# A hybrid RWKV-7 / pooling decoder block on one core: each step's leftover work queued behind the next weight split, GpSimd's DMAs in program order, and five products in 512/256-column pairs

## The chip, the cores and the metric

The kernel runs on one core of a Trainium2 chip. A core has TensorE (PE in the profile, its weight loads PEld), VectorE (DVE), ScalarE (ACT), GpSimd (POOL) and SyncE (SP), each with its own instruction queue, and 16 DMA engines that all of these queues feed. The metric is device microseconds of one execution, the median of the runs made.

## The reference, cut to what matters

One decoder block on a (1, 512, 2048) input in float32: 512 tokens, 2048 channels, 5632 hidden channels in the MLP (44 tiles of 128).

```python
h = _rmsnorm(x, norm1_g) * (1 + sc1) + sh1
p = h @ w_in                                  # RWKV-7 heads and pooling heads
mix = concat([rwkv7(p), pool(p)]) @ w_out
x = x + gt1 * mix
h = _rmsnorm(x, norm2_g) * (1 + sc2) + sh2
u = h @ w_up                                  # (512, 2 * 5632)
y = conv_b + sum_j conv_w[j] * shifted(u, j)  # causal, width 3
val, gate = split(y, 2)
x = x + gt2 * ((silu(gate) * val) @ w_down)
return _rmsnorm(x, norm_f_g)
```

The change is in the last part alone: `h @ w_up` ("up") and `... @ w_down` ("down"). Products are made to nearly full float32 precision: each operand is split into a rounded part and the rest ("hi" and "lo"), and hi·hi, hi·lo and lo·hi are summed.

## The kernel before

**A product.** `wsplit` (lines 1382 to 1390) splits a weight tile of 128 x 1024: ACT casts the hi part (line 1388), DVE subtracts to get the lo part (line 1389). There are three buffers for split weights, used in turn, so the hi cast of the third tile from now waits until PE is done with the present one. `mm3` (lines 132 to 150) then issues three matmuls for each 128 rows of the contraction: hi·hi (line 136), hi·lo (137), lo·hi (138). A product over 8 row tiles is 24 matmuls. With 256 columns (half of the tokens, `H0` or `H1`) they are called 128x256, with all tokens 128x512. `mm2` (lines 1217 to 1219), used in the output projection, instead issues two for each row tile: one of 512 columns with hi weights against hi and lo side by side, and one of 256 with lo weights. Its two halves of the PSUM bank are then added by whoever reads it.

**Up.** 44 pairs of output tiles, each a Strassen-Winograd 2 x 2 product of seven half-width products (`product`, line 1392). Thirty-four of the pairs form `w12 · Y21` themselves; `order` (line 1614) lists the pairs, and `n` is the place in that list. DVE is also used for the sums `r2`, `r4` and for the convolution, ACT for copies out of PSUM ("cap") and the activation.

**Down.** A list of steps (`Step`, line 1678) which `pipeline` (line 1683) runs: for step i it issues the step's matmuls, the weight load of step i+4, the split of step i+2, and then the step's `after` list (PSUM reads, operand preparation, stores, DMA loads). The framework's scheduler then orders the instructions of each engine by its own estimate; the program text is not the order. The steps are, in turn:
- 16 *plain* rows (`plain_steps`, line 1752): output tile f, first 8 hidden tiles, 24 matmuls of 512 columns; the last pair's open product is the second step. Beside them `operands` (line 1537) builds the Winograd operands Y11, Y21, Y22, T1, T2; `last_operand` builds T3 and T4 at the end of these rows, from the same buffers (xa, xb) that the second group's weights are loaded into.
- 8 *groups* f = 0..7 (`group_steps`, line 1781) over the next 16 hidden tiles, each of seven half-width steps of 24 matmuls: Y11, (T4 of the group before), Y21, T1, T2, Y22, T3. After them stand p1 to p7: p1 and p4 copy the first PSUM bank into `cap` (lines 1806 and 1816), p3 (line 1813) copies the second one, into which Y22 is then added, p2, p5 and p6 add on DVE, p7 copies on ACT; p5 and p7 also send the result to DRAM with an accumulating DMA from GpSimd's queue (lines 1820, 1830). The weights of a group are two loads of 1 MB on SP's queue (line 1779, `wd4`), issued by `pair_load`.
- *rest* rows (`rest_steps`) over the last 20 hidden tiles in blocks of 8, 8 and 4, first four rows block by block, then four rows, then two times eight rows of half width. Their activations are loaded by `rest_load` (line 1514; the first four by GpSimd's queue, the others by SP's) into the group operands' buffers as these come free, and split by `rest_split` (ACT line 1519, DVE line 1520). `fetch_x2` (lines 1905 and 1907) loads the residual and the sum stored so far on GpSimd's queue, `join_x2` (DVE, line 1910) adds them, `gate_row` (line 1890) makes the last modulation vector by DVE, `finish` writes the normalised output.

Of the kernel before, what the change touches and what calls it, by code (L numbers as in the profile page):

```python
# [1 line left out]

# [1 line left out]

# [5 lines left out]
F32 = mybir.dt.float32  # L10
# [3 lines left out]
ALU = mybir.AluOpType  # L14
PSUM = bass.MemoryType.PSUM

P = 128
T = 512
# [7 lines left out]
WC = 512  # L26
NWF = 8
NSLOT = 10
LA = 4
NB = 10  # L30
NA = 4
# [37 lines left out]
def block_kernel(ctx, tc, a, out, stop=None, dbg=None):  # L69
    nc = tc.nc  # L70
# [1139 lines left out]
    def bank():  # L1210
        return psm.tile([P, T], F32, tag="b", name="b")
# [20 lines left out]
    def x2(f, sl=slice(0, T)):  # L1232
        return x2q[f // 4][:, f % 4, sl]
# [143 lines left out]
        def done(self):  # L1377
            free.append(self.home)

    nsplit, lo_of = [0], [None]  # L1380

    def wsplit(src, off=0):
        n = src.shape[-1]
        i = nsplit[0] % 3
        nsplit[0] += 1
        w = (ea, ea, ub)[i].tile([P, WS], F32R, tag=f"w{i}", name="uw")
        hi, lo = w[:, off : off + n], w[:, 2 * QW + off : 2 * QW + off + n]
        S.copy(hi, src)  # L1388
        lo_of[0] = V.tensor_tensor(lo, src, hi.bitcast(F32), op=ALU.subtract)  # L1389
        return hi, lo  # L1390

    def product(ps, w, Y, start=True):
        wh, wl = wsplit(w, 16)
        n = w.shape[-1] // P
        for k in range(n):
            sl = slice(k * P, (k + 1) * P)
            y = Y[k // 4]
            mm3(ps, wh[:, sl], wl[:, sl], y[:, 0, k % 4, :], y[:, 1, k % 4, :], start=start and k == 0,
                stop=k == n - 1, more=not start)

    def row(n, pool, tag):
        t = pool.tile([P, 4 * QW], F32, tag=tag, name="wrow")
# [106 lines left out]
    def rest_load(i, eng):  # L1509
        u, g = REST[i]  # L1510
        pool, tag = UNITS[u][g]
        t = pool.tile([P, 2, 2, T], F32R, tag=tag, name="act2")
        for n in range(2):
            eng.dma_start(t[:, 1, n, :].bitcast(F32), ad[3 * ND + 2 * i + n])
        A3.extend([t[:, :, n, :] for n in range(2)])

    def rest_split(i):
# [99 lines left out]
    for n, j in enumerate(order):  # L1617
# [13 lines left out]
        if j < NB:  # L1631
            u1 = Slot("u1")
            nc.sync.dma_start(u1.t, early[j])
        else:
            product(pa, w11, Y11)
            S.copy(cap[:, H0], pa)
            if pend:
                last_product(pend)
            u1 = Slot("u1")
            pb = bank()[:, 0:HT]  # L1640
            product(pb, w12, Y21)
            V.tensor_add(u1[:, H0], cap[:, H0], pb)
        ahead_of_down(j)
        u2 = Slot("u2")
        pc = bank()[:, 0:HT]
# [37 lines left out]
    def pipeline(steps):  # L1683

        def ahead(i, what):
            if i < len(steps):
                what(steps[i])

        def load(st):
            if st.load:  # L1690
                st.load()

        def split(st):
            st.w = wsplit(st.raw(), st.off)

        for i in range(LA):
            ahead(i, load)
        ahead(0, split)
        ahead(1, split)
        carried = []  # L1700
        for i, st in enumerate(steps):
            st.mm(*st.w)
            ahead(i + LA, load)
            ahead(i + 2, split)
            todo, carried = carried + ([] if st.hold else st.after), st.after if st.hold else []
            for fn in todo:
                fn()

    def products(ps, wh, wl, Y, n, start=True):
        for k in range(n):  # L1710
# [70 lines left out]
    def group_steps():  # L1781

        out_, before = [], None
        for f in range(NWF):
# [42 lines left out]

            def p7(d=d, f=f):
                S.activation(d["u2"][:, H0], d["a"], AF.Copy, scale=-1.0)
                G.dma_start(yd[f + NWF], d["u2"].t, accum_op=ALU.add)  # L1830
                d["u2"].done()

            out_.append(Step(w11, mul(d, "a", "Y11"), [p1], off=16))
# [67 lines left out]
    def fetch_x2(f):  # L1901
        if not x2q:
            x2q.extend(quad(i, "x2") for i in range(4))
            accs.append(Slot("acc").t)
        G.dma_start(x2(f), x2d[f])
        parts[f] = Slot("yd")
        G.dma_start(parts[f].t, yd[f])

    def join_x2(f):
        V.scalar_tensor_tensor(x2(f), parts[f].t, gate(f), x2(f), op0=ALU.mult, op1=ALU.add)  # L1910
# [29 lines left out]
    for b, (k0, n) in enumerate(BLOCKS):  # L1940
        for f in range(4):
            st = four[f][0][b]
            steps.append(st)
            if b == 0 and f == 0:
                st.after += [lambda i=i: rest_load(i, nc.sync) for i in (4, 5)]
                before.after.append(gate_begin)
                steps.append(before)
            if b == 0 and f == 1:
                st.after += [lambda i=i: rest_load(i, nc.sync) for i in (6, 7)]
            if b == 0 and f == 2:  # L1950
                st.after += [lambda i=i: rest_split(i) for i in (4, 5)]
            if b == 0 and f == 3:
                st.after += [lambda i=i: rest_split(i) for i in (6, 7)] + [lambda i=i: rest_load(i, nc.sync) for i in (8, 9)]
# [135 lines left out]
```

## Time and profile before

| what | value |
|---|---|
| three runs | 2159.04, 2160.34, 2186.05 us; median 2160.34 us |
| the profiled execution: its own time | 2156.44 us |
| the profiled execution: its span in the trace | 2154.7 us (1.74 us less) |
| PE busy in the span | 2110.4 us, 98% |
| DVE, ACT, POOL busy | 78%, 49%, 11% |
| mean granted PE clock | 0.992 |
| up pairs run from about | 880 to 1668 us |
| plain rows, groups, rest rows from about | 1668, 1758 and 1916 us |
| last matmul of the rest rows, end | about 2138 us, 2154.7 us |

How to read it: a matmul record is longer than the distance to the next one, since matmuls overlap in the array; what a matmul costs is the distance of starts. In a window's row the number behind x is the count of instructions, PEclk the granted TensorE clock as a share of full speed, and in a timeline or wait row the bracket holds the engine's idle time before an instruction and what ended it.

### The profile page before, as it was taken

How to read it: one execution, taken by the hardware profiler on the slowest of the kernel's cores; microseconds unless marked ns; L12 is line 12 of the kernel's file. 1: busy time of each engine (PE TensorE's matmuls, PEld its weight loads, DVE VectorE, ACT ScalarE, POOL GpSimd, SP SyncE). 2: the span in 40 equal slices, each digit the busy share in tenths (PEclk: the TensorE clock that was granted, in tenths of full speed). 3: DMA queues.
4: the chain of work that ended last, by engine and by line, in shares of the span. 5: the costliest groups of instructions: out<-in, count | busy, mean ns of one | idle time of the engine just before them, and what ended most of it. 6: DMA issues, size and time to landing. Idle time of an engine off the chain costs nothing.

```text
span 2154.7 us, 44008 instructions
## 1 busy us (share of the span) xinstructions
PE 2110.4 (98%) x17864; PEld 1866.6 (87%) x17864; DVE 1677.5 (78%) x2615; ACT 1047.0 (49%) x1510; POOL 236.5 (11%) x376
## 2 busy tenths in 40 slices
PE   7999999999999999999999999999999999999997
PEld 3567777777767888999999999999999889988897
DVE  7988898988854677888888878777788657757764
ACT  4354444443433466655555555555556444443353
POOL 0002122221100101100100000000000000120000
PEclk9999999999999999999999999999999999999998
DMA  9966665665537565989889877777777635697855
GB/s 393 413 213 198 199 199 173 199 178 184 149 109 262 189 197 179 293 247 261 245 244 261 229 211 208 203 207 211 210 210 212 214 114 147 166 318 267 293 187 166
DMA packets 169485, 471.89 MB, mean 219 GB/s; under 512 B 21361, under 2 KB 29505, under 8 KB 159169
## 3 DMA queue, kind: packets, MB, share of 16 engines
q1 hardware_dynamic: 120370, 352.12, 48.0%
q0 software_dynamic: 27696, 79.20, 17.5%
q10 hardware_dynamic: 21216, 37.76, 5.8%
q8 instruction: 140, 2.29, 0.4%
q14 instruction: 63, 0.52, 0.1%
HBM read 432.81 MB, written 36.18 MB: 218 GB/s over the span
## 4 chain that ended last, share of the span: by engine, by line
PE 86%; DVE 5%; DMA 4%; ACT 2%; issue 2%; POOL 0%; DVEq 0%; ACTq 0%; POOLq 0%; SPq 0%
PE b L138 19%; PE b L136 19%; PE b L137 19%; PE mm L646 11%; PE pf L427 4%; PE b L1218 2%; PE b L1219 1%; DVE war L765 1%; PE pb L1048 1%; DMA wrow<-wup 1%; DMA war<-ada 1%; DMA wa<-ada 1%; PE pa L712 1%; DMA al<-ad 0%; ACT x L1318 0%
## 5 line engine op out<-in xcount | busy, mean ns | idle before, releaser
L138 PE MATMUL b<-t,uw 128*128 128x256 f32 x1408 | 388.6, 276 | 0.0
L136 PE MATMUL b<-t,uw 128*128 128x256 f32 x1408 | 388.6, 276 | 0.0
L137 PE MATMUL b<-t,uw 128*128 128x256 f32 x1408 | 388.6, 276 | 0.0
L136 PE MATMUL b<-y,uw 128*128 128x256 f32 x1056 | 293.2, 278 | 2.2 <-ACT uw L1388 2.2
L138 PE MATMUL b<-y,uw 128*128 128x256 f32 x1056 | 292.7, 277 | 0.9 <-DVE uw L1389 0.7
L646 PE MATMUL mm<-ahl,whi 128*128 128x512 f32 x864 | 290.6, 410 | 2.0 <-DVE rk L549 1.4
L137 PE MATMUL b<-y,uw 128*128 128x256 f32 x1056 | 292.5, 277 | 0.0
L137 PEld LDWEIGHTS b<-t,uw 128*128 128x128 f32 x1408 | 264.3, 188 | 0.0
L136 PEld LDWEIGHTS b<-t,uw 128*128 128x128 f32 x1408 | 264.3, 188 | 0.0
L138 PEld LDWEIGHTS b<-t,uw 128*128 128x128 f32 x1408 | 264.3, 188 | 0.0
L1389 DVE TENSOR_TENSOR uw<-r,uw 128x1024 fp32r<-128x1024 f32 x164 | 200.4, 1222 | 78.3 <-ACT uw L1388 78.3
L1389 DVE TENSOR_TENSOR uw<-wquart,uw 128x1024 fp32r<-128x1024 f32 x156 | 190.6, 1222 | 67.9 <-ACT uw L1388 67.5
L1389 DVE TENSOR_TENSOR uw<-wd,uw 128x1024 fp32r<-128x1024 f32 (+1 forms) x112 | 124.0, 1108 | 109.1 <-ACT uw L1388 109.1
L1388 ACT CAST uw<-wquart 128x1024 fp32r<-128x1024 f32 x156 | 164.0, 1051 | 88.3 <-PE b L138 65.3
L1388 ACT CAST uw<-r 128x1024 fp32r<-128x1024 f32 x164 | 172.5, 1052 | 61.2 <-PE b L138 61.1
L138 PE MATMUL b<-act,uw 128*128 128x256 f32 (+1 forms) x608 | 200.4, 330 | 1.4 <-DVE uw L1389 1.4
L136 PEld LDWEIGHTS b<-y,uw 128*128 128x128 f32 x1056 | 198.9, 188 | 2.8 <-ACT uw L1388 2.8
L136 PE MATMUL b<-act,uw 128*128 128x256 f32 (+1 forms) x608 | 200.6, 330 | 0.0
L138 PEld LDWEIGHTS b<-y,uw 128*128 128x128 f32 x1056 | 199.0, 189 | 1.7 <-DVE uw L1389 1.7
L137 PE MATMUL b<-act,uw 128*128 128x256 f32 (+1 forms) x608 | 200.4, 330 | 0.0
L137 PEld LDWEIGHTS b<-y,uw 128*128 128x128 f32 x1056 | 199.1, 189 | 0.1
L646 PEld LDWEIGHTS mm<-ahl,whi 128*128 128x128 f32 x864 | 158.8, 189 | 43.3 <-issue 12.2
(356 smaller groups left out, 4596.5 us busy)
## 6 DMA issues: line engine op xcount, KB each, us to landing
wquart<-wup SPq DMA_DIRECT2D x176, 512.0 KB, 5.3
wa<-ada SPq DMA_DIRECT2D x48, 1024.0 KB, 9.4
war<-ada SPq DMA_DIRECT2D x192, 256.0 KB, 3.8
wd<-wdn SPq DMA_DIRECT2D x64, 512.0 KB, 4.5
wraw<-win ACTq DMA_DIRECT2D x118, 256.0 KB, 4.1
wraw<-wout SPq DMA_DIRECT2D x96, 256.0 KB, 3.5
wquart<-wup POOLq DMA_DIRECT2D x44, 512.0 KB, 6.8
r<-wup SPq DMA_DIRECT2D x44, 512.0 KB, 4.6
```

The costliest lines, as they stand in the source:

```text
L136: muls = [lambda: PE.matmul(ps, wh, xh, start=start, stop=False, skip_group_check=more), lambda: PE.matmul(ps, wh, xl, start=False, stop=F ...
L137: lambda: PE.matmul(ps, wh, xl, start=False, stop=False, skip_group_check=more),
L138: lambda: PE.matmul(ps, wl, xh, start=False, stop=stop, skip_group_check=more)]
L427: PE.matmul(pf[n % 2 * 4 + ii], w[:, sl], full[k], start=k == 0, stop=k == KT - 1)
L646: PE.matmul(ps, w[:, sl], x, start=first, stop=k == KT - 1 and i == 2)
L712: PE.matmul(ps, pw[:, i, d * P : (d + 1) * P], zs[i], start=i == 0, stop=i == 1)
L765: V.scalar_tensor_tensor(wa, wa, 1.0, cqs[kq], op0=ALU.mult, op1=ALU.mult, accum_out=modq[:, kq, j : j + 1])
L1048: PE.matmul(pt[HS[e], h, c * 2 * L : (c + 1) * 2 * L], nt[HS[e], s, :], rw[HS[e], s, :, :], start=True, stop=True)
L1218: PE.matmul(ps[:, :].rearrange("p (a b) -> p a b", a=2), wh, x, start=start, stop=False)
L1219: PE.matmul(ps[:, 0:HT], wl, x[:, 0, :], start=False, stop=stop)
L1388: S.copy(hi, src)
L1389: lo_of[0] = V.tensor_tensor(lo, src, hi.bitcast(F32), op=ALU.subtract)
```

## The change

- In `pipeline`, everything in a step's `after` list is issued with an edge behind the hi cast and the lo subtraction of the last split made (that of step i+2): on ACT nothing of it stands before that cast, on DVE nothing before that subtraction. The edge orders instructions on the same engine; it is no wait on another one.
- All GpSimd DMAs of the down part go through `queue`, which puts each behind the one before it in program order.
- In five pairs (n = 0, 2, 6, 14, 28, which are j = 10, 11, 13, 17 and 28) the second product uses `mm2`: 8 matmuls of 512 columns and 8 of 256 instead of 24 of 256, and two DVE additions instead of one.

```diff
+WIDE = (0, 2, 6, 14, 28)
...
-        S.copy(hi, src)
+        hi_of[0] = S.copy(hi, src)
...
+    def product_wide(ps, w, Y):
+        wh, wl = wsplit(w, 16)
+        for k in range(w.shape[-1] // P):
+            sl = slice(k * P, (k + 1) * P)
+            mm2(ps, wh[:, sl], wl[:, sl], Y[k // 4][:, :, k % 4, :], k == 0, k == 7)
...
-            pb = bank()[:, 0:HT]
-            product(pb, w12, Y21)
-            V.tensor_add(u1[:, H0], cap[:, H0], pb)
+            pb = bank()
+            if n in WIDE:
+                product_wide(pb, w12, Y21)
+                V.tensor_add(u1[:, H0], cap[:, H0], pb[:, HT:T])
+                V.tensor_add(u1[:, H0], u1[:, H0], pb[:, 0:HT])
+            else:
+                product(pb[:, 0:HT], w12, Y21)
+                V.tensor_add(u1[:, H0], cap[:, H0], pb[:, 0:HT])
...
+    def queue(*args, **kw):
+        with tc.issue_after(g_of[0].ins) if g_of[0] else nullcontext():
+            g_of[0] = G.dma_start(*args, **kw)
...
-            for fn in todo:
-                fn()
+            with tc.issue_after(hi_of[0].ins), tc.issue_after(lo_of[0].ins):
+                for fn in todo:
+                    fn()
...
-        G.dma_start(yd[f], s_.t)
+        queue(yd[f], s_.t)
...
-                G.dma_start(yd[f], d["u1"].t, accum_op=ALU.add)
+                queue(yd[f], d["u1"].t, accum_op=ALU.add)
...
-        p[0].after += [lambda: rest_load(0, G), lambda: rest_load(1, G)]
-        p[2].after += [lambda: rest_load(2, G), lambda: rest_load(3, G)]
+        p[0].after += [lambda: rest_load(0, queue), lambda: rest_load(1, queue)]
+        p[2].after += [lambda: rest_load(2, queue), lambda: rest_load(3, queue)]
...
-        G.dma_start(x2(f), x2d[f])
+        queue(x2(f), x2d[f])
         parts[f] = Slot("yd")
-        G.dma_start(parts[f].t, yd[f])
+        queue(parts[f].t, yd[f])
```

Other GpSimd DMAs of the down part are changed in the same way. Lines of the changed kernel are 7 to 17 higher there. What this does to the built order is seen at three places. In the rows, `uw` is a split weight tile, the number behind a name tells buffers' uses apart.

**ACT, last group (f = 7) of the down part.** `b_21432` (before) and `b_21397` (changed) are the bank that p3 reads, `act2` the rest activations, `u2` p7 of group 6; r2, r4, r3 are the weights of T2, Y22 and T3. Before:

```order
L1388 CAST uw_21389<-r1_21387 128x1024
L1519 CAST act2_21357<-act2_21357 128x512 x2
L1829 ACTIVATE u2_21325<-b_21113 128x256
L1388 CAST uw_21421<-r2_21419 128x1024
L1519 CAST act2_21360<-act2_21360 128x512 x2
L1388 CAST uw_21461<-r4_21459 128x1024
L1519 CAST act2_21426<-act2_21426 128x512 x2
L1519 CAST act2_21429<-act2_21429 128x512
L1813 COPY cap_21355<-b_21432 128x256
L1388 CAST uw_21495<-r3_21493 128x1024
```

With the change:

```order
L1389 CAST uw_21354<-r1_21352 128x1024
L1846 ACTIVATE u2_21290<-b_21078 128x256
L1389 CAST uw_21386<-r2_21384 128x1024
L1389 CAST uw_21426<-r4_21424 128x1024
L1526 CAST act2_21322<-act2_21322 128x512 x2
L1830 COPY cap_21320<-b_21397 128x256
L1389 CAST uw_21460<-r3_21458 128x1024
L1526 CAST act2_21325<-act2_21325 128x512 x2
```

Ahead of p3's copy stood seven casts of rest activations, now two stand there, and p7 of group 6 (`u2`) stands ahead of all of them.

**GpSimd's queue at the same place.** `ad` are the rest activations in DRAM, `x2d` the residual. Before:

```order
L1820 DMA yd6_19188<-u1_21204 128x512
L1905 DMA x2_21801<-x2d8_7428 128x512
L1905 DMA x2_21801<-x2d9_7429 128x512
L1905 DMA x2_21801<-x2d10_7430 128x512
L1514 DMA act2_21357<-ad24_9801 128x512
L1514 DMA act2_21357<-ad25_9802 128x512
L1514 DMA act2_21360<-ad26_9803 128x512
L1514 DMA act2_21360<-ad27_9804 128x512
L1905 DMA x2_21801<-x2d11_7431 128x512
L1830 DMA yd14_19196<-u2_21325 128x512
L1514 DMA act2_21426<-ad28_9805 128x512
```

With the change:

```order
L1692 DMA yd6_19153<-u1_21169 128x512
L1692 DMA act2_21322<-ad24_9801 128x512
L1692 DMA act2_21322<-ad25_9802 128x512
L1692 DMA act2_21325<-ad26_9803 128x512
L1692 DMA act2_21325<-ad27_9804 128x512
L1692 DMA yd14_19161<-u2_21290 128x512
L1692 DMA act2_21391<-ad28_9805 128x512
```

The residual's loads have left the stretch ahead of the activations' loads; they now stand in pairs with the `yd` loads behind the last accumulating store.

**PE, ACT and DVE at the start of the second group (f = 1).** Before, PE goes from T3 of group 0 straight through Y11 of group 1 (`b_20043`), and ACT casts in the order Y11, T4, Y21:

```order
L137 MATMUL b_19834<-T3_19875,uw_19981 128x256
L138 MATMUL b_19834<-T3_19875,uw_19981 128x256
L136 MATMUL b_20043<-Y11_19370,uw_20009 128x256
L137 MATMUL b_20043<-Y11_19370,uw_20009 128x256
L138 MATMUL b_20043<-Y11_19370,uw_20009 128x256
```

```order
L1816 COPY cap_19878<-b_19834 128x256
L1388 CAST uw_20009<-wd4_19920 128x1024
L1388 CAST uw_20038<-wd4_19681 128x1024
L1388 CAST uw_20068<-wd4_19920 128x1024
L1806 COPY cap_20071<-b_20043 128x256
```

With the change, on PE, on ACT and on DVE (`wd4_19885` is the load with the weights of Y11 and Y21 of group 1, `r2_20094` a sum for its T2):

```order
L139 MATMUL b_19799<-T3_19840,uw_19946 128x256
L137 MATMUL b_20008<-Y11_19335,uw_19974 128x256
L138 MATMUL b_20008<-Y11_19335,uw_19974 128x256
L137 MATMUL b_20069<-Y21_19338,uw_20033 128x256
L138 MATMUL b_20069<-Y21_19338,uw_20033 128x256
L139 MATMUL b_20008<-Y11_19335,uw_19974 128x256
```

```order
L1833 COPY cap_19843<-b_19799 128x256
L1389 CAST uw_20003<-wd4_19646 128x1024
L1389 CAST uw_19974<-wd4_19885 128x1024
L1389 CAST uw_20033<-wd4_19885 128x1024
L1823 COPY cap_20036<-b_20008 128x256
```

```order
L1809 TENSOR_TENSOR r1_20062<-wd4_19887 128x1024
L1390 TENSOR_TENSOR uw_20003<-wd4_19646,uw_20003 128x1024
L1809 TENSOR_TENSOR r2_20094<-r1_20062,wd4_19885 128x1024
L1390 TENSOR_TENSOR uw_19974<-wd4_19885,uw_19974 128x1024
L1836 TENSOR_TENSOR u1_19880<-cap_19843,b_19889 128x256
```

T4's weights (`uw_20003`) are now split ahead of Y11's (`uw_19974`) on both engines, and two matmuls of Y21 (`b_20069`) stand between the second and the third matmul of Y11. DVE's order further ahead has the parts of T3 and T4 later than before: the subtraction of T4's second half, which frees the buffer of `wd4_19885`, stands behind the split of T2's weights and p2 of group 0:

```order
L1390 TENSOR_TENSOR uw_19829<-r1_19827,uw_19829 128x1024
L1539 TENSOR_TENSOR T3_19835<-t3_19448,T3_19835 128x512
L1539 TENSOR_TENSOR T3_19835<-t3_19450,T3_19835 128x512
L1809 TENSOR_TENSOR r3_19944<-wd4_19644,wd4_19646 128x1024
L1539 TENSOR_TENSOR T3_19840<-xb_19293,T3_19840 128x1024
L1539 TENSOR_TENSOR T4_19845<-t4_19489,T4_19845 128x512
L1539 TENSOR_TENSOR T4_19845<-t4_19491,T4_19845 128x512
L1390 TENSOR_TENSOR uw_19877<-r2_19875,uw_19877 128x1024
L1827 TENSOR_TENSOR u1_19880<-cap_19843,b_19850 128x256
L1539 TENSOR_TENSOR T4_19882<-xa_19292,T4_19882 128x1024
```

Before, T4's last subtraction was done ahead of the split of T2's weights, and five of the others ahead of the split of T1's.

More of the change, by code (lines that the diff above doesn't have):

```diff
@@ L1 @@
-from contextlib import ExitStack
+from contextlib import ExitStack, nullcontext
 import numpy as np
@@ L1378, in done @@
             free.append(self.home)
[L1380 removed]
+    nsplit, lo_of, hi_of, g_of = [0], [None], [None], [None]
     def wsplit(src, off=0):
@@ L1829, in p7 @@
                 S.activation(d["u2"][:, H0], d["a"], AF.Copy, scale=-1.0)
-                G.dma_start(yd[f + NWF], d["u2"].t, accum_op=ALU.add)
+                queue(yd[f + NWF], d["u2"].t, accum_op=ALU.add)
                 d["u2"].done()
@@ L1944, in block_kernel @@
             if b == 0 and f == 0:
-                st.after += [lambda i=i: rest_load(i, nc.sync) for i in (4, 5)]
+                st.after += [lambda i=i: rest_load(i, nc.sync.dma_start) for i in (4, 5)]
                 before.after.append(gate_begin)
@@ L1948, in block_kernel @@
             if b == 0 and f == 1:
-                st.after += [lambda i=i: rest_load(i, nc.sync) for i in (6, 7)]
+                st.after += [lambda i=i: rest_load(i, nc.sync.dma_start) for i in (6, 7)]
             if b == 0 and f == 2:
@@ L1952, in block_kernel @@
             if b == 0 and f == 3:
-                st.after += [lambda i=i: rest_split(i) for i in (6, 7)] + [lambda i=i: rest_load(i, nc.sync) for i in (8, 9)]
+                st.after += [lambda i=i: rest_split(i) for i in (6, 7)] + [lambda i=i: rest_load(i, nc.sync.dma_start) for i in (8, 9)]
             if b == 1 and f in (0, 2):
```

2 lines of the change are left out of this document (1 added, 1 removed).

## The prediction

> **What bounds the kernel now.** The page first: who is busy, and which chain of work ended last.
>
> ```profile
> PE 2110.4 (98%) x17864; PEld 1866.6 (87%) x17864; DVE 1677.5 (78%) x2615; ACT 1047.0 (49%) x1510; POOL 236.5 (11%) x376
> PE 86%; DVE 5%; DMA 4%; ACT 2%; issue 2%; POOL 0%; DVEq 0%; ACTq 0%; POOLq 0%; SPq 0%
> ```
>
> TensorE is busy nearly throughout. A change of order can therefore bring only the places where PE stands still or runs at a lower clock, and can cost only where it makes new ones. So next the waits of PE, of which three rows lie in the up and down parts:
>
> ```profile
> PE b L136 <- ACT cap L1813: 4.6, 1, 4.6
> PE b L136 <- ACT uw L1388: 2.2, 3, 1.0
> PE b L138 <- DVE uw L1389: 2.1, 2, 1.4
> ```
>
> The columns are total us, times, longest. The longest of the third row is where the plain rows begin, the first row is in the last group. Windows show both, the stretch behind the second, and some that I need for prices:
>
> ```profile
> core 0: us, PE busy (x) PEld busy (x) DVE busy (x) ACT busy (x) POOL busy (x), PEclk, DMA share, GB/s
> 740.00:790.00 50.00, 50.00 (x286) 43.47 (x285) 35.60 (x65) 25.78 (x46) 4.67 (x9) 1.00 0.66 209
> 853.00:856.00 3.00, 1.52 (x9) 1.11 (x8) 3.00 (x4) 2.11 (x3) 0.03 (x1) 0.94 0.95 352
> 856.00:859.00 3.00, 3.00 (x16) 3.00 (x16) 3.00 (x4) 0.00 (x0) 1.43 (x2) 0.50 0.67 184
> 868.00:871.00 3.00, 1.55 (x9) 1.11 (x9) 3.00 (x4) 1.89 (x2) 0.54 (x1) 1.00 0.97 395
> 900.00:1600.00 700.00, 700.00 (x6179) 700.00 (x6178) 575.53 (x673) 389.26 (x506) 69.05 (x79) 1.00 0.83 227
> 1660.00:1670.00 10.00, 8.61 (x72) 8.13 (x71) 8.76 (x11) 8.12 (x13) 0.00 (x0) 1.00 0.74 220
> 1690.00:1750.00 60.00, 60.00 (x266) 49.71 (x265) 27.01 (x25) 19.03 (x25) 5.98 (x12) 1.00 0.46 161
> 1908.00:1914.00 6.00, 5.91 (x28) 5.91 (x29) 4.04 (x6) 4.97 (x10) 0.00 (x0) 0.52 0.99 373
> ```
>
> In a window without waits, 256-column matmuls start every 700/6179 = 0.1133 us and those of 512 columns every 60/266 = 0.2256 us. Everything below is priced against these.
>
> **Part 1: the wait at the first plain row.** DVE, then ACT, at 1660 to 1670 us:
>
> ```profile
> 1665.99 0.41 DVE L1662 TENSOR_TENSOR u<-cap,b 128x256 f32<-128x256 f32 x1
> 1667.65 0.69 DVE L1505 TENSOR_TENSOR act<-al,act 128x512 fp32r<-128x512 f32 x1 [1.24 <-ACT act L1504]
> 1668.26 1.22 DVE L1389 TENSOR_TENSOR uw<-wd,uw 128x1024 fp32r<-128x1024 f32 x1
> ```
>
> ```profile
> 1664.06 1.06 ACT L1388 CAST uw<-wd 128x1024 fp32r<-128x1024 f32 x1
> 1667.00 0.62 ACT L1504 CAST act<-al 128x512 fp32r<-128x512 f32 x1 [1.88 <-DMA al<-ad]
> ```
>
> The hi half was ready at 1665.1, but DVE's lo half stood behind a subtraction whose activation came late by DMA. In the changed order that lo half stands ahead of it, and DVE was free at 1666.4. **−1.39 us** (10 − 8.61). Bounds: −1.39 (nothing is left to gain) and 0, if the late activation then holds up the next row's lo half; I take the whole, since this row's 24 matmuls give 24 × 0.2256 = 5.4 us of cover.
>
> **Part 2: the wait in the last group.** PE, ACT and POOL:
>
> ```profile
> 1908.09 0.58 PE L136 MATMUL b<-Y,uw 128*128 128x256 f32 x1 [4.63 <-ACT cap L1813]
> ```
>
> ```profile
> 1896.02 1.31 ACT L1519 CAST act<-act 128x512 fp32r<-128x512 f32 x2 [2.08 <-DMA act<-ad]
> 1897.24 0.38 ACT L1829 ACTIVATE u<-b 128x256 f32<-128x256 f32 x1
> ...
> 1899.78 1.04 ACT L1388 CAST uw<-r 128x1024 fp32r<-128x1024 f32 x1
> 1905.03 0.62 ACT L1519 CAST act<-act 128x512 fp32r<-128x512 f32 x1 [4.21 <-DMA act<-ad]
> ...
> 1907.15 0.62 ACT L1519 CAST act<-act 128x512 fp32r<-128x512 f32 x1 [0.39 <-DMA act<-ad]
> 1907.67 0.37 ACT L1813 COPY cap<-b 128x256 f32<-128x256 f32 x1
> ```
>
> ```profile
> 1889.78 1.64 POOL L1905 DMA_DIRECT2D x<-x2d  x3 [0.96 <-DVE uw L1389]
> 1891.52 1.09 POOL L1514 DMA_DIRECT2D act<-ad  x2
> ...
> 1897.91 0.89 POOL L1830 DMA_DIRECT2D yd<-u  x1 [3.41 <-ACT u L1829]
> 1898.48 2.48 POOL L1514 DMA_DIRECT2D act<-ad  x4
> ```
>
> The circle reads: Y22's first matmul waits for p3's copy; that copy stands behind three casts whose loads arrive at 1905 to 1907; the loads were issued at 1898.48, behind the store of p7, which waited for the ACT copy at 1897.24, which in turn stood behind casts that waited for the first loads. With the change p7's copy stands ahead of all these casts. It needs only its bank and can run about 2 us earlier, near 1895.3, so the last two pairs' loads are issued at about 1896.7 to 1899. The first four loads start about 1.5 us earlier, the three x2d issues (1.64 us) no longer being ahead of them. Ahead of p3's copy now stand the split of Y22's weights and two casts, both of the first pair (issued near 1891.5, landing some 4 us later). The copy then comes at about 1900.8 and Y22 needs it at 1903.46. **−4.63 us.** Bounds: −4.63, and 0 if those two casts still end last. I take the former; 2.7 us lie between copy and need.
>
> **Part 3: the clock behind it.** In 1908:1914 PE ran 28 matmuls in 5.91 us at a granted clock of 0.52; at the normal pitch these take 28 × 0.1133 = 3.17. **−2.74 us**, if the wait goes; 0 if it stays.
>
> The Trainium skill, "TensorE: Matmul & The Clock Gate", section "Part 1: The HAM clock gate (the "warmup" mystery)", has the clock fall to half after an idle window of about 3.4 us and return after about 3.4 us of activity. This trace differs twice: low clock lasted some 5.5 us here, and it also came in 856:859 when only 1.48 of the 3 us ahead were idle. By the page's 3.4 us this term would be an estimated −1.7 rather than −2.74.
>
> **Part 4: a wait that the new order makes.** At f = 1 the changed order lets three things come late. T4's subtraction (`T<-xa`), which frees the buffer of the next load of weights, moves behind the split of T2's weights. Then T4's split stands ahead of Y11's on ACT and DVE, and on DVE a sum (`r2`) that needs the late load also stands ahead of Y11's lo half. Before, DVE and ACT had there:
>
> ```profile
> 1763.16 1.22 DVE L1532 TENSOR_TENSOR T<-xa,T 128x1024 fp32r<-128x1024 f32 x1
> ...
> 1771.87 1.23 DVE L1792 TENSOR_TENSOR r<-r,wd 128x1024 f32<-128x1024 f32 x1 [1.80 <-DMA wd<-wdn]
> 1773.02 1.22 DVE L1389 TENSOR_TENSOR uw<-wd,uw 128x1024 fp32r<-128x1024 f32 x1
> ```
>
> ```profile
> 1764.41 0.33 SPq L1779 DMA_DIRECT2D wd<-wdn  x1
> ```
>
> ```profile
> DMA to landing us min/median/max: 4.9/6.0/7.4
> ```
>
> ```profile
> 1771.86 2.13 ACT L1388 CAST uw<-wd 128x1024 fp32r<-128x1024 f32 x2 [1.22 <-DMA wd<-wdn]
> ```
>
> ```profile
> 1775.46 0.28 PE L136 MATMUL b<-Y,uw 128*128 128x256 f32 x1
> ```
>
> T3 of group 0 ends and Y11 of group 1 begins at 1775.46. In the changed order `T<-xa` ends about 1769, the load is issued then instead of at 1764.41, and lands 6.0 us later at about 1775.1. `r2` then runs 1775.2 to 1776.4, Y11's lo half up to 1777.55. In PE's order only two matmuls of Y11 and two of Y21 stand ahead of the one that needs that lo half, 4 × 0.1133 = 0.45 us, up to 1775.91. So PE stands still 1777.6 − 1775.91 = **+1.7 us**. With a landing of 4.9 `r2` is ready at 1774.0 and only T4's own lo half (1774.05 to 1775.28) precedes: 0.6 us; with 7.4 it is +2.9. Below that 0, if `T<-xa` comes earlier than I reckon. I take the median's. T4's split needs the third buffer back from Y22, whose end leaves 1.3 us for its cast; that is met in either order.
>
> **Part 5: five wide products.** The price is in the output projection, where pairs of 512 and 256 columns run: 50 us / 143 pairs = 0.3497 per pair, against 3 × 0.1133 = 0.3399. Difference 0.0098 × 8 row tiles × 5 products = **+0.39 us**. From the other side, single matmuls give 0.2256 + 0.1133 = 0.3389, so −0.04. I take the pair's row, the nearest. The five extra additions on DVE (below, 413 ns each, 2.1 us) fall where DVE idles for ACT's casts:
>
> ```profile
> L1389 DVE TENSOR_TENSOR uw<-wquart,uw 128x1024 fp32r<-128x1024 f32 x156 | 190.6, 1222 | 67.9 <-ACT uw L1388 67.5
> ...
> L1642 DVE TENSOR_TENSOR u<-cap,b 128x256 f32<-128x256 f32 x34 | 14.1, 413 | 0.1
> ```
>
> Without that cover they would cost up to 5 × 0.41 = 2.1 us.
>
> **Part 6: what moves at no cost.** All other steps' leftovers (PSUM reads, operand casts, stores, SP's loads) shift by at most a split, 1.22 us on DVE, behind work that PE needs one or two products later (24 × 0.1133 = 2.7 us each). The edges make no engine wait for another; what lies behind them is read a step later. On POOL's queue x2d and yd loads now come in pairs behind the last accumulating store, near 1917; the first join is needed later than that. After the last matmul (2138 us) nothing moves.
>
> **Sum**, in the profiled execution: −1.39 − 4.63 − 2.74 + 1.7 + 0.39 = −6.67 us, 2156.44 → 2149.8. That execution lies 3.9 us below the median of the runs, 2160.34; carried over, the forecast is **2153.7 us**. By the terms' bounds: lowest −8.76 − 0.04 = −8.8, so 2151.5; highest with all chosen gains and the dear ends +2.9 and +2.5, −3.4, so 2157.0. With a run's scatter of 0.5 us its own range is 2151 to 2157.5.
>
> **The rivals.** *A dip at f = 1.* For it: 1.48 us of idle in 853:856 was followed by half clock (16 matmuls in 3 us, 3 − 16 × 0.1133 = 1.19 us lost). Against it: 1.45 us idle in 868:871 brought none, nor did 1.39 at 1668 us. With a landing of 7.4 (+1.2) and a dip of 1.2 to 2.7: about 2156.8 us.
>
> *The last group's wait stays.* Two casts of loaded activations still stand ahead of p3's copy. If the first pair of loads lands some 6 us later than reckoned, behind the group's weight loads (the engines' DMA share is 0.99 there), ACT is held as before, the copy is late and the clock falls: +4.63 + 2.74, so 2161.1 us, slightly slower than before.
>
> *Strict order on GpSimd's queue delays the joins.* A yd load waits for a slot that the previous join frees:
>
> ```profile
> POOL yd L1907 <- DVE x L1910: 59.8, 8, 15.1
> ```
>
> Before, an x2d load of the next row could go ahead of such a wait; now it queues behind, so a join may find its residual not there and hold the splits behind it on DVE. It decides once a load takes longer than the distance from slot to join; at about 1 us for each of 12 rows, 2165.7 us. Against it: the slot was waited for up to 15.1 us, so rows are far apart.
>
> *No wait at f = 1*, since DVE reaches `T<-xa` a step earlier: 2152.0 us.
>
> **How the numbers follow.** Forecast 0.5, dip at f = 1 0.2, last group's wait stays 0.1, joins late 0.1, no wait at f = 1 0.1. The range 2146 to 2164 us holds all but the late joins and half of what scatters beyond the others, about 8 in 10. Two per cent, 43 us, is about what a measurement of this kernel can tell from no change. No case comes near it: faster 0.01, same 0.97, slower 0.02 (joins that stall for 4 us a row).
>
> **What would show it.** Right: no row of PE waiting for p3's copy; full clock behind 1900 us; one new wait of 1 to 3 us for a lo split 110 us behind the first plain row; pairs in the wide products near 0.35 us. Wrong: PE waiting in the groups f = 2 to 7, in the rest rows for a split held by a join, or in the up part behind the extra additions.

## The result, and the profile after

| | before | changed |
|---|---|---|
| median of 9 runs each | 2160.34 us | 2184.24 us |
| lowest to highest | 2156.03 to 2190.92 us | 2182.59 to 2191.46 us |
| profiled execution: own time, span | 2156.44, 2154.7 us | 2186.87, 2185.1 us |

The ratio is 1.0104, with a 95% interval of 1.0069 to 1.0139. The forecast of 2153.7 us was missed by 30.5 us and the end of its range (2164) by 20: the change was to save some 7 us and costs about 24, or 1%. One thing in these rows matters for what follows: two of the nine runs of before lie at 2186 and 2191 us, in the band of the changed kernel, and not one run of the changed kernel lies lower.

The page of the changed kernel, the rows of busy time and of the chain:

```profile
PE 2141.0 (98%) x17824; PEld 1895.1 (87%) x17824; DVE 1683.4 (77%) x2620; ACT 1044.5 (48%) x1510; POOL 236.2 (11%) x376
PE 83%; issue 6%; DVE 4%; DMA 4%; ACT 2%; POOL 1%; POOLq 0%; ACTq 0%; DVEq 0%; SPq 0%
```

PE is busy 30.6 us longer than before with 40 matmuls fewer. So the loss is not a wait. The waits of PE in the up and down parts confirm it: the row of p3's copy is gone, and what is left adds up to 7.7 us, part of which stands ahead of the up part (below).

```profile
PE b L137 <- ACT uw L1389: 6.8, 5, 4.3
PE b L139 <- DVE uw L1390: 0.9, 2, 0.7
```

Windows of the changed kernel, for the same stages as in the prediction, which lie 30 to 38 us later from the first plain row on (the last number of a row is GB/s, the one behind the three shares of engines the granted clock):

```profile
core 0: us, PE busy (x) PEld busy (x) DVE busy (x) ACT busy (x) POOL busy (x), PEclk, DMA share, GB/s
900.00:1600.00 700.00, 700.00 (x5914) 698.51 (x5913) 560.70 (x654) 373.65 (x487) 67.64 (x78) 1.00 0.80 219
1702.00:1712.00 10.00, 10.00 (x59) 8.78 (x58) 6.56 (x8) 6.09 (x10) 0.57 (x1) 1.00 0.83 264
1720.00:1780.00 60.00, 60.00 (x267) 49.67 (x266) 37.01 (x33) 25.72 (x32) 5.94 (x11) 1.00 0.49 162
1805.00:1812.00 7.00, 5.39 (x43) 4.85 (x42) 5.16 (x6) 3.04 (x3) 0.00 (x0) 1.00 0.61 212
1812.00:1816.00 4.00, 4.00 (x23) 4.00 (x23) 2.58 (x3) 0.00 (x0) 0.89 (x1) 0.57 0.63 150
1924.00:1940.00 16.00, 16.00 (x143) 16.00 (x143) 11.78 (x14) 8.52 (x12) 6.18 (x10) 1.00 0.69 176
1940.00:1946.00 6.00, 6.00 (x55) 6.00 (x55) 5.71 (x8) 5.12 (x9) 0.90 (x1) 1.00 1.05 410
```

The first row is the result. In 900:1600 PE never stood still and its granted clock was full, in both kernels. Before, 6179 matmuls fitted into these 700 us; now 5914. Four wide products lie in the window, and each has 8 instructions fewer, so the count to compare is 5914 + 32 = 5946. 700/5946 = **0.1177 us** from start to start, where it was 0.1133. Nearly all 256-column matmuls of the up part are slower, not only those of the wide products. The rows of 512 columns are as before (60/267 = 0.2247 us), and in 1924:1940 the 256s of the last groups are back at 16/143 = 0.112 (the border of so short a window adds one to the count).

The two profiled executions differ by 30.4 us. The starts of the same matmuls in both split this up: 0.9 us ahead of 837 us and 3.0 between 837 and 882 us, most of it in longer waits, where nothing was edited; 30.8 from there to the first plain row, which is the pace (6930 instructions x 0.0044 = 30.5) and the little that the wide pairs cost themselves; -1.7 at the first plain row; +4.5 at f = 1; -7.6 in the last group with its clock; 0.4 behind the last matmul.

### The profile page after: what moved, and what is told of

The parts are those of the page before. It is cut to its first block, busy times and chain, and to the rows that moved or that the text cites. A ratio compares the mean times of both kernels' runs of the same rounds, so it can differ in the third digit from the quotient of the medians.

```text
span 2185.1 us, 43937 instructions
## 1 busy us (share of the span) xinstructions
PE 2141.0 (98%) x17824; PEld 1895.1 (87%) x17824; DVE 1683.4 (77%) x2620; ACT 1044.5 (48%) x1510; POOL 236.2 (11%) x376
## 4 chain that ended last, share of the span: by engine, by line
PE 83%; issue 6%; DVE 4%; DMA 4%; ACT 2%; POOL 1%; POOLq 0%; ACTq 0%; DVEq 0%; SPq 0%
PE b L138 18%; PE b L137 18%; PE b L139 18%; PE mm L647 11%; PE pf L428 4%; PE b L1219 2%; PE b L1220 1%; DMA wrow<-wup 1%; DVE war L766 1%; PE pb L1049 1%; PE pa L713 1%; DMA wa<-ada 1%; ACT x L1319 0%; DMA wraw<-win 0%; PE pf L138 0%
## 5 line engine op out<-in xcount | busy, mean ns | idle before, releaser
L139 PE MATMUL b<-t,uw 128*128 128x256 f32 x1408 | 395.6, 281 | 0.0
L138 PE MATMUL b<-t,uw 128*128 128x256 f32 x1408 | 395.6, 281 | 0.0
L137 PE MATMUL b<-t,uw 128*128 128x256 f32 x1408 | 395.6, 281 | 0.0
L137 PE MATMUL b<-y,uw 128*128 128x256 f32 x1016 | 286.9, 282 | 5.2 <-ACT uw L1389 5.2
L139 PE MATMUL b<-y,uw 128*128 128x256 f32 x1016 | 285.9, 282 | 0.8 <-DVE uw L1390 0.7
L138 PE MATMUL b<-y,uw 128*128 128x256 f32 x1016 | 286.1, 282 | 0.0
L137 PEld LDWEIGHTS b<-y,uw 128*128 128x128 f32 x1016 | 195.7, 193 | 5.9 <-ACT uw L1389 5.9
L139 PEld LDWEIGHTS b<-y,uw 128*128 128x128 f32 x1016 | 191.7, 189 | 1.2 <-DVE uw L1390 1.2
L138 PEld LDWEIGHTS b<-y,uw 128*128 128x128 f32 x1016 | 192.1, 189 | 0.1
```

What stands on the lines that cost most here:

```text
L137: muls = [lambda: PE.matmul(ps, wh, xh, start=start, stop=False, skip_group_check=more), lambda: PE.matmul(ps, wh, xl, start=False, stop=F ...
L138: lambda: PE.matmul(ps, wh, xl, start=False, stop=False, skip_group_check=more),
L139: lambda: PE.matmul(ps, wl, xh, start=False, stop=stop, skip_group_check=more)]
```

## The experiments

All kernels below are edits of the changed kernel or of before; each ratio is to runs of before made beside it.

**Which part of the change slows the matmuls?** Four kernels: the new order without wide products, wide products without the new order, and a single wide product, early or late.

```diff
-WIDE = (0, 2, 6, 14, 28)
+WIDE = ()        # order_only
+WIDE = (0,)      # wide_first
+WIDE = (28,)     # wide_late
```

> The changed kernel without its five wide products. Theory 1 (a 512/256 product leaves TensorE in a slower pace, 0.1177 us from start to start of 256-column matmuls in place of 0.1133, which then holds until the array is next interrupted): the up part runs at 0.1133 again and the time falls by some 6900 x 0.0043 = 30 us, to about 2154 us. Theory 2 (the pace is set by the wait ahead of the up part, near 870 us, and the wide products have no share in it): runs at 2154 and at 2184 us mixed, as with the kernel before, where 2 runs of 9 were near 2188. Theory 3 (the new order itself slows the matmuls): 2184 us in all runs.

> The kernel before with the five wide products alone. Theory 1: the whole up part behind the first one at 0.1177, about 2160 + 30 = 2190 us in all runs. Theory 2: mixed, mostly 2160.7 us. Theory 3: 2160.7 us, that is before plus the 0.4 us of the pairs.

> The changed kernel with one wide product, that of n = 0, 16 matmuls of 17824. Theory 1: as slow as with all five, 2184 us, since the pace that it leaves holds to the end of the up part. If each wide product costs by itself: a fifth of the 30 us, 2160 us. Theory 2: mixed.

> The changed kernel with one wide product, that of n = 28, at about 1360 us. Theory 1: 0.1133 up to it, 0.1177 behind it; some 2620 matmuls of 256 columns are left in the up part, 2620 x 0.0043 = 11 us, so about 2165 us. If each wide product costs by itself: 2160 us, with one pace on both sides of it. Theory 2: one pace from 880 us to the end of the up part, either.

| kernel | runs, us | ratio, 95% interval |
|---|---|---|
| order_only | 7 of 10 in 2151.7 to 2164.9, 3 in 2180.6 to 2186.2 | 0.9976 (0.9921 to 1.0031) |
| wide_only | 4 of 4 in 2186.9 to 2192.0 | 1.0105 (1.0031 to 1.0180) |
| wide_first | 10 of 10 in 2182.7 to 2192.2 | 1.0111 (1.0081 to 1.0142) |
| wide_late | 6 of 10 in 2163.6 to 2169.8, then 2176.8, 2181.2, 2182.5, 2188.2 | 1.0019 (0.9970 to 1.0069) |

The order is cleared and the wide products are guilty, but not by their own cost: one of them, 16 matmuls, costs as much as five. The late one costs about a third, in the runs that began in the quicker pace. The timeline of wide_first shows the moment. The rows give start and duration of each matmul; the wide product is lines 1219 and 1220:

```profile
896.38 0.28 PE L137 MATMUL b<-y,uw 128*128 128x256 f32 x1
896.49 0.28 PE L138 MATMUL b<-y,uw 128*128 128x256 f32 x1
896.60 0.28 PE L139 MATMUL b<-y,uw 128*128 128x256 f32 x1
896.72 0.39 PE L1219 MATMUL b<-y,uw 128*128 128x512 f32 x1
896.94 0.28 PE L1220 MATMUL b<-y,uw 128*128 128x256 f32 x1
897.06 0.40 PE L1219 MATMUL b<-y,uw 128*128 128x512 f32 x1
897.30 0.28 PE L1220 MATMUL b<-y,uw 128*128 128x256 f32 x1
...
899.42 0.28 PE L1220 MATMUL b<-y,uw 128*128 128x256 f32 x1
899.53 0.28 PE L137 MATMUL b<-t,uw 128*128 128x256 f32 x1
899.65 0.28 PE L138 MATMUL b<-t,uw 128*128 128x256 f32 x1
899.77 0.28 PE L139 MATMUL b<-t,uw 128*128 128x256 f32 x1
899.89 0.28 PE L137 MATMUL b<-t,uw 128*128 128x256 f32 x1
```

Ahead of the first 512 the starts are 0.11 us apart (0.1133 over many), behind it 0.118, and so it stays for 6840 matmuls, to the first plain row: no wait, full clock. In wide_late the same happens at n = 28:

```profile
900.00:1350.00 450.00, 450.00 (x3973) 450.00 (x3972) 380.44 (x452) 250.91 (x321) 47.17 (x54) 1.00 0.86 239
1380.00:1680.00 300.00, 300.00 (x2549) 300.00 (x2548) 230.76 (x263) 161.96 (x218) 24.43 (x28) 1.00 0.75 203
```

450/3973 = 0.1133 ahead of it, 300/2549 = 0.1177 behind it. So there are **two paces of the same stream of matmuls**, each holds until something disturbs it, and a wide product sets the slower one. Theories 2 and 3 fall. Theory 2 has a share, though: the profiled execution of order_only (2181.6 us) ran the up part at 700/5946 = 0.1177 without a wide product, from its first matmuls at full clock behind the wait at 870 us on. A restart of PE can catch either pace. The profiled execution of the changed kernel is such a case as well: its matmuls are 0.118 us apart from 877 us on, ahead of the first wide product at 893.84. So the two profiles of the result show that the pace is the loss, but not what set it; that is shown by wide_first and wide_late, where the pace changes at the wide product, and by the counts of runs in the table.

```profile
900.00:1600.00 700.00, 700.00 (x5946) 700.00 (x5945) 559.61 (x650) 374.56 (x487) 66.89 (x77) 1.00 0.80 220
```

**What can bring the quicker pace back?** One kernel with many forms of the product. Those that begin the halves of a bank apart add up other sums than the reference's; the matmuls and their places are as told.

```diff
+VAR = {0: 'w', 2: 'a', 4: 'w', 6: 'b', 8: 'w', 10: 'c', 12: 'w', 14: 'd', 16: 'w', 18: 'e', 20: 'w', 21: 'f',
+       22: 'w', 23: 'g', 24: 'w', 25: 'h', 26: 'w', 27: 'k', 28: 'w', 29: 'l', 30: 'w', 31: 'm', 32: 'w', 33: 'e'}
...
-                product_wide(pb, w12, Y21)
+                product_var(v, pb, pb2, w12, Y21)
```

> The changed kernel with the second product of w12 in other forms in many pairs, to read from the starts of the matmuls which pace each form leaves behind. Wide products as in the change at n = 0, 4, 8, 12, 16, 20, 22, 24, 26, 28, 30, 32, which by theory 1 set the slow pace (0.1177) each time; between them one other form each: n = 2 all eight 512s and then all eight 256s; n = 6 the 256 ahead of the 512 of its row tile; n = 10 only the first row tile wide; n = 14 only the last; n = 29 only the fourth; n = 31 the second, fourth and sixth; n = 18 and 33 no wide one, but the first 256 cut into two of 128 columns; n = 21 the last 256 cut into two of 128; n = 25 the first cut into 64 and 192; n = 27 the last cut so; n = 23 the 256s of a wide product into a PSUM bank of their own. Theory 1a: any 512 followed by a 256 leaves the slow pace, and a cut matmul, which shifts the weight loads against the matmuls, can bring back the fast one (0.1133) until the next wide product. Theory 1b: nothing but a stop of the array ends the slow pace, so 0.1177 behind all of them. If neither the wide form nor the cuts matter: one pace all through, or changes that do not follow the list.

Theory 1a: behind each of the five products with a cut matmul (n = 18, 21, 25, 27, 33; first or last, 128 + 128 or 64 + 192) the pace was 0.1133, and the next wide product, where one followed, set 0.1177 again. One form without a cut did the same, which theory 1a does not allow: the eight 512s in one block (n = 2, from 926.95 us on). The starts are 0.1178 us apart ahead of it and 0.1133 behind it, until the wide product at n = 4; in windows of equal length:

```profile
900.00:925.00 25.00, 25.00 (x215) 25.00 (x214) 20.99 (x25) 14.02 (x19) 3.52 (x4) 1.00 0.94 256
930.00:955.00 25.00, 25.00 (x223) 25.00 (x222) 22.18 (x28) 14.63 (x19) 3.47 (x4) 1.00 0.85 221
```

The other six forms left 0.1177, but they also started from it, which this kernel cannot tell apart.

**Do the waits come and go with the parts named?** Three kernels without wide products: the edges without the operands of f = 1, the edges without the queue, the queue without the edges.

```diff
             for fn in todo:
-                fn()
+                if fn in loose:        # order_f1: last_operand("T3"), last_operand("T4"), pair_load(1)
+                    fn()
...
-        with tc.issue_after(g_of[0].ins) if g_of[0] else nullcontext():
-            g_of[0] = G.dma_start(*args, **kw)
+        G.dma_start(*args, **kw)       # edges_only
...
-            with tc.issue_after(hi_of[0].ins), tc.issue_after(lo_of[0].ins):
-                for fn in todo:
-                    fn()
+            for fn in todo:            # queue_only
+                fn()
```

> The changed kernel without wide products, and with the parts of T3 and T4 and the load of the weights of f = 1 left out of the edges, so that T4's last part, the load behind it and the split of Y11 stand as in the kernel before. The prediction's fourth term (the late load and the split of T4 ahead of Y11's make a wait at f = 1, and the clock can fall behind it): no wait of TensorE between Y11 and Y21 of f = 1 and full clock there, 2 to 4 us less than without the repair, about 2150 us in runs of the fast pace. Rival: the wait comes from the edges on other work, and stays.

> The changed kernel without wide products and without the strict order of GpSimd's DMAs: the edges behind the splits alone. If the edges take the wait in the last group away (p3's copy ahead of the late casts): no wait of 4 to 5 us on the copy, whatever GpSimd's order. If the queue's order does it (loads ahead of the residual's): the wait stays here. The wait at the first plain row goes, that at f = 1 comes.

> The kernel before with the strict order of GpSimd's DMAs alone. If the edges are what takes the last group's wait away: the wait of 4 to 5 us on p3's copy and the half clock behind it stay, or shrink by the 1.6 us of the residual's issues. If the queue does it: gone. The wait of 1.4 us at the first plain row stays, none at f = 1.

order_f1: 8 of 10 runs in 2147.2 to 2154.0 us and two near 2182, ratio 0.9960 (0.9949 to 0.9970), so it is quicker than before. PE has no wait at f = 1, and its window there is full:

```profile
1770.00:1790.00 20.00, 20.00 (x178) 20.00 (x178) 16.28 (x16) 9.46 (x13) 1.77 (x2) 1.00 0.50 137
```

edges_only has no wait on p3's copy at all. queue_only keeps most of it, here in its PE row at Y22, and keeps the one at the first plain row (longest of 1.7 us):

```profile
1907.89 0.39 PE L137 MATMUL b<-Y,uw 128*128 128x256 f32 x1 [2.93 <-ACT cap L1829]
```

So the edges take both old waits away, and the edges bring the new one; the queue's order alone shortens one wait, from 4.63 to 2.93 us. The other traces agree: of the kernels without the edges, before_cut (below) and wide_only keep the wait in the last group (3.57 and 4.54 us), and none with the edges has it. For the first plain row edges_only is weak evidence, since it ran in the slower pace, and in that pace wide_only has no wait there without the edges; order_f1, in the quicker pace, has none with them. edges_only and queue_only are single runs, so their totals (2181.36 and 2154.7 us) say only which pace they caught.

**The cut as a cure.** If pace is the whole loss, a cut matmul behind each wide product must give it back, and cuts early in the up part must remove the runs near 2185 us of any kernel here.

```diff
+            if cut and k == n - 1:
+                PE.matmul(ps, wh[:, sl], xh, start=False, stop=False, skip_group_check=True)
+                PE.matmul(ps, wh[:, sl], xl, start=False, stop=False, skip_group_check=True)
+                for h in (slice(0, HT // 2), slice(HT // 2, HT)):
+                    PE.matmul(ps[:, h], wl[:, sl], xh[:, h], start=False, stop=True, skip_group_check=True)
+                continue
...
-        product(pc, r1, T1)
+        product(pc, r1, T1, cut=n in (0, 1, 2))   # best (on order_f1), before_cut
+        product(pc, r1, T1, cut=n in WIDE)        # wide_cut (on the change)
```

> The changed kernel without wide products, with the parts of T3 and T4 and the load of the weights of f = 1 outside the edges, and with the last matmul of the T1 product cut into two of 128 columns in the pairs n = 0, 1, 2. Theory 1 with 1a (a 512/256 product sets the slow pace, a cut matmul the fast one, and each holds until the array is interrupted): all runs in the fast pace, 2147 to 2152 us, none near 2182, where 2 of 10 were without the cuts. Rival (the cuts of the probe stood near an unseen cause): runs near 2182 appear again, at a rate of 2 to 4 in 10.

> The changed kernel with all five wide products, and in the same five pairs the last matmul of the T1 product, the one behind the wide product, cut into two of 128 columns. Theory 1 with 1a: the slow pace lasts only from each wide product to the cut behind it, 24 matmuls; 2184 - 30 = about 2154 us in all runs, so the wide products cost nothing but the pace. Rival (the wide products cost their time in another way, or the fast pace cannot come back): stays at 2184 us or at some level between.

> The kernel before with the cuts at n = 0, 1, 2 alone. If its own runs of 2185 to 2195 us are the slow pace, caught at the interruptions ahead of the up part: they vanish, all runs at 2155 to 2163 us. If they are something else: they stay, about 1 run in 4.

| kernel | median, lowest to highest, runs | ratio, 95% interval |
|---|---|---|
| wide_cut | 2154.21, 2152.07 to 2162.65, 10 | 0.9985 (0.9956 to 1.0014) |
| before_cut | 2157.95, 2155.90 to 2160.70, 10 | 0.9994 (0.9968 to 1.0021) |
| best | 2150.23, 2148.45 to 2156.84, 12 | 0.9960 (0.9934 to 0.9987) |

Five matmuls cut in two take 30 us from the changed kernel. Of 77 runs of before in all comparisons 20 lay above 2175 us; of the 32 runs in this table none did. The window of the kernel called best:

```profile
900.00:1600.00 700.00, 700.00 (x6178) 700.00 (x6178) 576.33 (x673) 388.05 (x505) 69.47 (x80) 1.00 0.82 227
```

It beats both kernels, before by 0.4%: the new order with the operands of f = 1 outside the edges, no wide products, three cuts.

**Which part of a wide product sets the pace?** Seven forms in seventeen pairs, each from the quicker pace, as a cut precedes it.

```diff
+VAR = {0: 'w', 2: 'a', 4: 'b', 6: 'c', 8: 'g', 10: 'x', 12: 'e', 14: 'w', 16: 'a', 18: 'b', 20: 'c', 22: 'g',
+       24: 'x', 26: 'e', 28: 'w', 30: 'x', 31: 'c'}
...
-        product(pc, r1, T1)
+        product(pc, r1, T1, cut=n in VAR)
```

> Which part of a wide product sets the slow pace: the changed kernel with one form of the second product in each of 17 pairs, and the last matmul of the T1 product behind it cut into two of 128 columns, so that each form starts from the fast pace. Forms: as in the change (n = 0, 14, 28); eight 512s, then eight 256s (2, 16); the 256 ahead of the 512 (4, 18); only the first row tile wide, then 256s (6, 20); the first three row tiles wide (12, 26, and 31 as 6); the 256s into a bank of their own (8, 22); as in the change with the last 256 cut into two of 128 (10, 24, 30). Theory 1a in its strict form: any 512 followed by a 256 leaves 0.1177, whatever the length, order or bank; the form that ends in a cut leaves 0.1133. Rival: the alternation over eight row tiles is needed, and forms with one wide row tile, or with the 512s in one block, stay at 0.1133. In all forms the time of the whole kernel is near 2155 us, as the slow pace lasts 24 matmuls.

One wide row tile (n = 6), and the eight 512s in one block (n = 2), with the first 256s of the next product in each:

```profile
990.20 0.28 PE L139 MATMUL b<-t,uw 128*128 128x256 f32 x1
990.32 0.28 PE L140 MATMUL b<-t,uw 128*128 128x256 f32 x1
990.43 0.39 PE L1414 MATMUL b<-y,uw 128*128 128x512 f32 x1
...
993.25 0.28 PE L138 MATMUL b<-t,uw 128*128 128x256 f32 x1
993.37 0.28 PE L139 MATMUL b<-t,uw 128*128 128x256 f32 x1
993.48 0.28 PE L140 MATMUL b<-t,uw 128*128 128x256 f32 x1
993.60 0.28 PE L138 MATMUL b<-t,uw 128*128 128x256 f32 x1
```

```profile
925.12 1.56 PE L1414 MATMUL b<-y,uw 128*128 128x512 f32 x6
926.52 1.07 PE L1418 MATMUL b<-y,uw 128*128 128x256 f32 x8
927.43 0.28 PE L138 MATMUL b<-t,uw 128*128 128x256 f32 x1
927.54 0.28 PE L139 MATMUL b<-t,uw 128*128 128x256 f32 x1
927.66 0.28 PE L140 MATMUL b<-t,uw 128*128 128x256 f32 x1
927.77 0.28 PE L138 MATMUL b<-t,uw 128*128 128x256 f32 x1
```

| form, from the quicker pace | pairs | pace behind it |
|---|---|---|
| as in the change | 3 of 3 | 0.1177 |
| 256 ahead of the 512 | 2 of 2 | 0.1177 |
| only the first row tile wide | 3 of 3 | 0.1177 |
| the first three wide | 2 of 2 | 0.1177 |
| 256s into their own bank | 2 of 2 | 0.1177 |
| eight 512s, then eight 256s | 2 of 2 | 0.1133 |
| as in the change, last 256 cut | 3 of 3 | 0.1133 |

A single 512 among 256s is enough; order and bank don't matter; a block of eight does no harm. Theory 1a in its strict form (any 512) is wrong, and so is the rival (the alternation is needed). Inside the block the starts are by turns 0.236 and 0.231 us apart. It would be tempting to say that each 512 shifts the stream once and an even number brings it back, but then the block at n = 2 of the kernel probe, which began in the slower pace, would have left it, and it left the quicker one. No block of another length was tried, so what the block does stays open.

Every trace holds a warning against a simple rule for the single 512, too. Where the plain rows end, 256s and 512s alternate three times behind 357 512s in a row (in before from 1758.43 to 1759.24 us), and once more behind 453 of them at 2027 us. There the quicker pace follows, in all 14 traces; in before:

```profile
1759.50:1774.50 15.00, 15.00 (x134) 15.00 (x133) 11.88 (x13) 8.56 (x11) 0.54 (x1) 1.00 0.65 229
```

So what a 512 leaves depends on what stood before it.

## Why the prediction failed, point by point

**Part 5 is the step that failed**: "five wide products ... +0.39 us", at a price per pair, with everything "priced against" 0.1133. The pairs themselves cost little more than that: from start to start 0.118 + 0.235 = 0.353 us, so 0.5 us for all forty against the quicker pace. What was missing is what they leave behind: 30 us. The term assumed that the spacing of back-to-back matmuls is a property of their shape. It is a property of shape and history.

The traces and times of before held two warnings. One of its three runs lay at 2186.05 us and I took it for scatter of no meaning; the range was worked out with a scatter of 0.5 us. And behind the first plain row, where 512s end and a product of 256s begins, its own timeline reads:

```profile
1674.43 0.39 PE L138 MATMUL b<-act,uw 128*128 128x512 f32 x1
1674.66 0.28 PE L136 MATMUL b<-t,uw 128*128 128x256 f32 x1
...
1675.25 0.28 PE L138 MATMUL b<-t,uw 128*128 128x256 f32 x1
```

Five steps in 0.59 us, 0.118 each, at full clock: the slower pace, set by 512s, in a place where it lasts only 24 matmuls. A mean over 700 us hides that there is a second value.

**Parts 1 to 3 were right.** Both waits are gone, with the clock behind the second at 1.00 in 1940:1946: by the starts -1.7 us at the first plain row and -7.6 us in the last group, where the three parts had -1.39 and -7.37. The chain of part 2 came as told. p3's copy waited for its bank alone, and ran 37.5 us later than the forecast 1900.8, just as much as the whole stage had moved:

```profile
1938.32 0.37 ACT L1830 COPY cap<-b 128x256 f32<-128x256 f32 x1 [0.58 <-PE b L139]
```

I had credited the GpSimd order and the edges together; the runs give it to the edges.

**Part 4 had the place and the cause, and was too small.** ACT, DVE and SP of the changed kernel around f = 1:

```profile
1806.47 1.05 ACT L1389 CAST uw<-wd 128x1024 fp32r<-128x1024 f32 x1 [2.30 <-PE b L139]
1809.22 1.99 ACT L1389 CAST uw<-wd 128x1024 fp32r<-128x1024 f32 x2 [1.70 <-DMA wd<-wdn]
```

```profile
1807.56 1.23 DVE L1390 TENSOR_TENSOR uw<-wd,uw 128x1024 fp32r<-128x1024 f32 x1 [0.75 <-ACT uw L1389]
1809.29 1.23 DVE L1809 TENSOR_TENSOR r<-r,wd 128x1024 f32<-128x1024 f32 x1 [0.51 <-DMA wd<-wdn]
1810.43 1.22 DVE L1390 TENSOR_TENSOR uw<-wd,uw 128x1024 fp32r<-128x1024 f32 x1
```

The load was issued at 1802.37 us, 1768.8 in the times of before, where about 1769 was reckoned. It took 6.83 us to land, where the sum had 6.0, and so already the hi cast of Y11 waited for it (ACT, 1.70 us), which the sum left out, and not only `r2`. PE waited 1.16 and 0.45 us, and the clock then fell: 23 matmuls in 4 us at 0.57. From the start of the groups to the end of the dip 165 matmuls took 23.16 us where 165 x 0.1133 = 18.70 would do: **4.5 us** against the forecast 1.7, and within the rival "a dip at f = 1" (4.1 to 5.6). So here the rival happened. The waits are there in all eight kernels with the edges other than order_f1 and best; the clock fell in three of them (behind 1.61 us of waits here, 2.20 in wide_cut and 2.24 in wide_late) and not in the other five (0.95 to 1.85 us). The Trainium skill, "TensorE: Matmul & The Clock Gate", section "Part 1: The HAM clock gate (the "warmup" mystery)", asks for an idle window of about 3.4 us before the clock falls; the trace has the fall behind waits of 1.61 us in all.

**Part 6 held but for a trifle.** No wait for a join or for GpSimd's queue reached PE. One split came late: at 1800.93 us PE waited 0.17 us for T1's lo half, which stood on DVE behind parts of T3 and T4; it is in the 4.5 us. The rivals "the last group's wait stays" and "joins late" did not happen.

Without the pace the total looks nearly right: wide_cut, the change with the pace restored, has a median of 2154.21 us against the 2153.7 forecast. Part of that agreement is luck. Term 4 was too small, and the runs of before made beside wide_cut have a median of 2158.56 us, so the saving there is 4.4 us where 6.67 was forecast; its interval, 0.9956 to 1.0014, even holds no change at all.

## What to carry to other kernels

Before pricing a matmul of another shape inside a long uninterrupted stream, look at the start-to-start distances on both sides of the places where that shape occurs already; if they differ at full clock, the price is the whole stream behind it and not the instruction. One such place isn't enough: before had the slower pace behind the 512s at 1674.66 us and the quicker one behind those at 1758.43. Read a lone outlier among the times as a second way in which the kernel can run, and ask what decides between them. When an order edge is added to everything that follows a step, exempt what starts a load that the next stage waits for.

## What the runs showed of the hardware

- Streams of 128x256 float32 matmuls, each with its weight load, ran in one of two paces at full clock and without waits: 0.1133 or 0.1177 us. Either held for thousands of matmuls (6930 in before, 6840 in wide_first). The Trainium skill, page "TensorE: Matmul & The Clock Gate", section "Back-to-back issue gap", has a formula for the gap of an isolated matmul, by which 256 columns come to an estimated 0.109 us, and says that in a stream weight load and matmul set the spacing together. The trace has two values, both above that estimate.
- A lone 512, one to eight times in a stream of 256s, set the slower pace (12 of 12 from the quicker one). Three 512s that alternated with 256s behind hundreds of 512s in a row were followed by the quicker one (two places in each of 14 traces), and a direct change to 256s behind 24 512s by the slower one (two places in each).
- A 256 cut into 128 + 128 or 64 + 192 set the quicker pace every time. A stop of PE led to either: the waits at f = 1 left the quicker one in the changed kernel and the slower one in wide_first (60 us / 512 matmuls = 0.1172 behind them).
- A block of eight 512s was followed by the quicker pace whatever stood ahead: 2 of 2 from the quicker one, and the only one tried from the slower.
- Why there are two paces isn't settled: no run here looks into it. That the weight loads and the matmuls lock in one of two phases is only a guess.
